# The SSD's decays between tokens: two float32r products over split log decays in place of one float32 product

## Chip, core and metric

The kernel runs on one core of a Trainium2 chip. The metric is the device time of one execution in microseconds (us), lower is better; the time before is the median of three runs. A profiled execution is taken beside these.

## The reference

A two-layer backbone over 1024 latent tokens and 256 context tokens, width 1024. Layer 0 has differential attention beside RWKV-7, layer 1 a bidirectional Mamba-2 SSD beside a bidirectional gated linear attention (GLA); each layer ends with a squared-ReLU MLP. What matters here is the SSD's chunk, of 128 tokens, for 8 heads and both directions:

```python
cum = jnp.cumsum(lac, axis=1)                       # log decays, summed along the tokens
lmat = jnp.exp(jnp.where(lower, cum[:, :, None] - cum[:, None, :], -jnp.inf))
cb = jnp.einsum('bign,bjgn->bijg', cc, bc)
xdt = xc * dtc[..., None]
y = jnp.einsum('bijgr,bjgrp->bigrp', cb[..., None] * lmat, xdt)
y = y + jnp.einsum('bign,bgrpn->bigrp', cc, h) * jnp.exp(cum)[..., None]
w_end = jnp.exp(cum[:, -1:] - cum)
h = h * jnp.exp(cum[:, -1])[..., None, None] + jnp.einsum('bjgn,bjgrp->bgrpn', bc, xdt * w_end[..., None])
```

`lmat` holds the decay between each two tokens: the exponential of the sum of the log decays that lie between them.

## The kernel before

Activations lie feature-major, 128 partitions wide. The large projections and the MLPs run as three float32r products of high and low parts (`mm3`, L87 to L89), with weights split on ACT (L95) and POOL (L99). Layer 1 goes in this order: projections with the SSD's convolution; the set-up of the SSD's log decays (`Ssd.dts`, about 2528 us), which fills `la`, one column per chunk, head and direction; the GLA's scores and its scan (`Gla.scan`, L1448 to L1497); the SSD's scan (`Ssd.scan`); the GLA's post-processing (`Gla.post`); the output projection `wout1`; the MLP. These stages overlap: the order of the instructions on each engine is planned when the kernel is built, by a list scheduler that uses its own cost model (`schedule_with_timeline_sim=True`), and then is fixed; each engine works through its own queue in order.

The SSD's scan takes nine or ten steps per direction over the chunks. A step updates the state (`xw` and the decayed state on POOL, L1176 and L1183; the product on PE, L1180; the sum on DVE, L1185), adds the part of the earlier chunks to the output (`inter`, L1244), and for each of the eight latent chunks calls `intra` (L1194) once. `intra` makes the decays between the tokens of the chunk in a PSUM tile `pd`, once for each group `g` of four heads, summed over both directions `d`. For a direction ACT writes `rl`, the mask `upto` or `from` scaled by the head's log decays (four instructions, L1221), and PE multiplies it by the mask `after` or `before` (L1222), a float32 product of 128x128 by 128x512. Then ACT takes the exponential (`G`, L1224), DVE multiplies by the masked scores (`us`, L1227) and PE multiplies by the values (L1232). That is 8 x 2 x 2 = 32 products at L1222 and 128 instructions at L1221. `rl` has two buffers.

`Gla.post` (L1499) runs through eight units. Each is a chain: squares on ACT (L1508), their sums on PE (L1511), an inverse square root by Newton steps on DVE (`rsqrt_newton`, L115 to L122), a broadcast on PE (L1515), two products on DVE (L1516, L1517) and a split on ACT and POOL. One PSUM buffer, `si`, carries both products of a unit.

`split` (L91) writes the high part by a copy that rounds to float32r and the low part as the difference.

## Time and profile before

| | |
|---|---|
| median of three runs | 3973.41 us (3969.83 to 3978.0) |
| the profiled execution | 3967.53 us |
| its span | 3965.7 us |
| PE busy | 3587.8 us, 90% of the span |
| DVE busy | 2048.2 us, 52% |
| POOL busy | 1305.6 us, 33% |
| ACT busy | 1138.8 us, 29% |
| mean granted TensorE clock | 0.935 of full speed |

The span runs from the first to the last instruction; the execution's time has 1.8 us more around it. Busy shares are means over stages with different limits, so the stage in which the changed lines run, about 2867 to 3056 us, is to be read by itself. A granted clock of 1.00 is 2.4 GHz, one of 0.50 is 1.2 GHz.

### The profile page before, as it was taken

The numbers are of one execution on the slowest core, as the hardware profiler recorded it, in microseconds if no ns is written. First come the engines' busy times: TensorE is split into PE (matmuls) and PEld (weight loads), VectorE is DVE, ScalarE is ACT, GpSimd is POOL, SyncE is SP. The second block draws the span as 40 slices with busy tenths as digits, with TensorE's granted clock in tenths as the row PEclk, the third lists the DMA queues.
The fourth block names the chain that finished last, engine by engine and source line by source line (L and its number), as shares of the span: only waits on it lengthen the run. The fifth ranks groups of instructions, "written<-read, shape, count | busy, mean of one in ns | idle before, by whom it ended". The sixth has DMA issues, their size and how long they took to land.

```text
span 3965.7 us, 68983 instructions
## 1 busy us (share of the span) xinstructions
PE 3587.8 (90%) x28912; PEld 2976.9 (75%) x28912; DVE 2048.2 (52%) x3741; ACT 1138.8 (29%) x1926; POOL 1305.6 (33%) x1121
## 2 busy tenths in 40 slices
PE   6999967766778879999999999999998889999998
PEld 4878846665667668888888888778776778888886
DVE  6344435766657647555444436357247663333335
ACT  3333321111255505111111113575543141111112
POOL 2455532322310015233222323217434352333223
PEclk8999977787788989999999999999999889999998
DMA  5244462333262142122222212232442311111111
GB/s 199 79 122 127 118 188 85 111 109 114 81 187 78 51 146 68 59 85 75 71 68 85 75 38 77 67 92 70 121 126 84 109 54 43 46 56 48 43 43 64
DMA packets 288999, 353.14 MB, mean 89 GB/s; under 512 B 91825, under 2 KB 217265, under 8 KB 288561
## 3 DMA queue, kind: packets, MB, share of 16 engines
q1 hardware_dynamic: 288688, 348.74, 28.3%
q8 instruction: 227, 3.72, 0.4%
q14 instruction: 84, 0.68, 0.1%
HBM read 265.03 MB, written 83.62 MB: 88 GB/s over the span
## 4 chain that ended last, share of the span: by engine, by line
PE 58%; DVE 3%; DMA 1%; ACT 1%; issue 1%; POOL 0%; SPq 0%; POOLq 0%; ACTq 0%; DVEq 0%
PE mm L87 10%; PE mm L88 10%; PE mm L89 10%; PE ss L87 4%; PE ss L88 4%; PE ss L89 4%; PE sp L88 4%; PE sp L87 4%; PE sp L89 4%; PE sp L1222 1%; PE ss L1475 1%; PE sp L1406 1%; PE si L1491 1%; PE mm L1232 1%; DMA wraw<-in_wout_dram 0%
## 5 line engine op out<-in xcount | busy, mean ns | idle before, releaser
L88 PE MATMUL mm<-actl,whi 128*128 128x512 f32 (+1 forms) x2432 | 903.3, 372 | 18.6 <-DVE actl L298 10.8
L87 PE MATMUL mm<-acth,whi 128*128 128x512 f32 (+1 forms) x2432 | 899.8, 372 | 19.2 <-ACT acth L95 6.9
L89 PE MATMUL mm<-acth,wlo 128*128 128x512 f32 (+1 forms) x2432 | 892.8, 370 | 0.0
L99 POOL TENSOR_TENSOR wlo<-wraw,whi 128x1024 fp32r<-128x1024 f32 (+2 forms) x243 | 495.7, 2047 | 1072.7 <-ACT whi L95 1065.4
L87 PEld LDWEIGHTS mm<-acth,whi 128*128 128x128 f32 x2432 | 465.1, 191 | 112.9 <-issue 8.1
L88 PEld LDWEIGHTS mm<-actl,whi 128*128 128x128 f32 x2432 | 465.3, 191 | 107.9 <-DVE actl L298 11.9
L89 PEld LDWEIGHTS mm<-acth,wlo 128*128 128x128 f32 x2432 | 465.0, 191 | 81.9 <-issue 4.4
L95 ACT CAST whi<-wraw 128x1024 fp32r<-128x1024 f32 (+2 forms) x243 | 217.1, 906 | 1049.5 <-PE mm L88 386.0
L345 POOL TENSOR_TENSOR relu<-relu 128x256 f32<-128x256 f32 (+1 forms) x163 | 162.2, 995 | 368.8 <-ACT relu L344 368.8
L97 DVE CAST hidh<-relu 128x256 fp32r<-128x256 f32 (+1 forms) x163 | 71.1, 436 | 354.8 <-POOL relu L345 353.6
L88 PE MATMUL sp<-hidl,whi 128*128 128x512 f32 (+1 forms) x648 | 238.5, 368 | 1.5 <-DVE hidl L99 1.5
L344 ACT ACTIVATE relu<-mm 128x256 f32<-128x256 f32 (+1 forms) x163 | 88.9, 545 | 520.8 <-PE mm L89 378.7
L87 PE MATMUL sp<-hidh,whi 128*128 128x512 f32 (+1 forms) x648 | 238.3, 368 | 0.0
L89 PE MATMUL sp<-hidh,wlo 128*128 128x512 f32 (+1 forms) x648 | 238.0, 368 | 0.0
L87 PE MATMUL ss<-hidh,whi 128*128 128x512 f32 (+1 forms) x600 | 222.8, 371 | 0.4 <-DVE hidh L97 0.4
L88 PE MATMUL ss<-hidl,whi 128*128 128x512 f32 (+1 forms) x600 | 222.5, 371 | 0.2 <-DVE hidl L99 0.2
L89 PE MATMUL ss<-hidh,wlo 128*128 128x512 f32 (+1 forms) x600 | 221.8, 370 | 0.0
L369 DVE SCALAR_TENSOR_TENSOR x<-ss,g,x 128x256 f32<-128x256 f32 x180 | 118.9, 661 | 145.2 <-PE ss L89 145.2
L369 DVE SCALAR_TENSOR_TENSOR x<-sp,g,x 128x512 f32<-128x512 f32 (+1 forms) x192 | 126.8, 661 | 105.5 <-PE sp L89 105.4
L220 DVE CUSTOM_DVE_ANT_0 mdj<-mdw,silu_r,t_cols 128x1024 f32<-128x1024 f32 x128 | 172.7, 1349 | 1.2
L369 DVE SCALAR_TENSOR_TENSOR x<-ss,g2b,x 128x512 f32<-128x512 f32 x120 | 90.0, 751 | 142.6 <-PE ss L89 142.6
L369 DVE SCALAR_TENSOR_TENSOR x<-sp,g2b,x 128x512 f32<-128x512 f32 (+1 forms) x132 | 96.7, 733 | 101.9 <-PE sp L89 101.9
(510 smaller groups left out, 6636.0 us busy)
## 6 DMA issues: line engine op xcount, KB each, us to landing
mdw<-in_modt_dram SPq DMA_DIRECT2D x80, 512.0 KB, 3.6
wraw<-in_wa_dram SPq DMA_DIRECT2D x64, 512.0 KB, 3.6
wraw<-in_wb_dram SPq DMA_DIRECT2D x64, 512.0 KB, 3.5
wraw<-in_win_dram SPq DMA_DIRECT2D x51, 512.0 KB, 3.8
x<-in_xT_dram SPq DMA_DIRECT2D x16, 640.0 KB, 10.7
rw_kr<-rw_t SPq DMA_DIRECT2D x16, 640.0 KB, 3.3
rw_bk<-rw_t SPq DMA_DIRECT2D x32, 320.0 KB, 3.9
rkr<-rw_kr SPq DMA_DIRECT2D x20, 512.0 KB, 5.1
```

Source lines behind the costliest of these rows:

```text
L87: self.nc.tensor.matmul(out, lh, rh, start=start and i == 0, stop=False)
L88: self.nc.tensor.matmul(out, lh, rl, start=False, stop=False)
L89: self.nc.tensor.matmul(out, ll, rh, start=False, stop=stop and i == n - 1)
L95: nc.scalar.copy(out=hi, in_=src)
L97: nc.vector.tensor_copy(out=hi, in_=src)
L99: e.tensor_tensor(out=lo, in0=src, in1=hi.bitcast(F32), op=ALU.subtract)
L220: nc.vector.tensor_tensor_reduce(out=junk, in0=raw, in1=rows[:, j], scale=1.0, scalar=modb[:, 8 * w + t : 8 * w + t + 1], op0=ALU.mult, op ...
L344: nc.scalar.activation(out=r, in_=ps, func=AF.Relu)
L345: nc.gpsimd.tensor_tensor(out=r, in0=r, in1=r, op=ALU.mult)
L369: nc.vector.scalar_tensor_tensor(out=xg, in0=ps, scalar=gate[:, m, j : j + 1], in1=xg, op0=ALU.mult, op1=ALU.add)
L1222: nc.tensor.matmul(pd, k["after" if d == 0 else "before"], rl.rearrange("p h t -> p (h t)"), start=d == 0, stop=d == 1)
L1232: nc.tensor.matmul(o, xd[d][:, hd * 64 : hd * 64 + 64], us[hd // 4, d][:, hd % 4], start=d == 0, stop=d == 1)
```

## The change

In the set-up `la` is split into a high part `lah`, rounded to float32r, and a low part `lal`, the rest, both as float32r tiles; the masks `after` and `before` are copied into float32r tiles `past[0]` and `past[1]`. In `intra` each `rl` becomes two tiles: the high one is written by ACT as before, with `lah` in place of `la`, and the low one by one GpSimd multiply of the mask with `lal`, over all four heads at once. Each float32 product then becomes two float32r products, of the high and of the low tile, added up in the same `pd`. Both new tiles have two buffers.

```diff
@@ Ssd.dts
+        self.lah, self.lal = (keep.tile([P, 10, 16], F32R, name=f"ss_la{x}") for x in "hl")
+        n.split(self.lah, self.lal, self.la)
+        self.past = [keep.tile([P, P], F32R, name=f"ss_past{d}") for d in range(2)]
+        for d in range(2):
+            nc.vector.tensor_copy(out=self.past[d], in_=k["after" if d == 0 else "before"])
+
@@ Ssd.intra
             for d in range(2):
-                rl = T([P, 4, P], "srl", 2)
+                rl = [self.pool.tile([P, 4, P], F32R, name=f"srl{x}", tag=f"srl{x}", bufs=2) for x in "hl"]
                 col = 8 * d + 4 * g
                 for r in range(4):
-                    nc.scalar.activation(out=rl[:, r], in_=tri[d], func=AF.Copy, scale=self.la[:, w + 2, col + r : col + r + 1])
-                nc.tensor.matmul(pd, k["after" if d == 0 else "before"], rl.rearrange("p h t -> p (h t)"), start=d == 0, stop=d == 1)
+                    nc.scalar.activation(out=rl[0][:, r], in_=tri[d], func=AF.Copy, scale=self.lah[:, w + 2, col + r : col + r + 1].bitcast(F32))
+                nc.gpsimd.tensor_tensor(out=rl[1], in0=tri[d].unsqueeze(1).to_broadcast([P, 4, P]),
+                                        in1=self.lal[:, w + 2, col : col + 4].bitcast(F32).unsqueeze(2).to_broadcast([P, 4, P]), op=ALU.mult)
+                for q, t in enumerate(rl):
+                    nc.tensor.matmul(pd, self.past[d], t.rearrange("p h t -> p (h t)"), start=d + q == 0, stop=d + q == 2)
```

## Rows read from the trace of the kernel before

**Rows 1.** The top of the page: the span and all instructions.

```profile
span 3965.7 us, 68983 instructions
```

**Rows 2.** Windows of the stage around the SSD's scan, every engine's busy time. Columns: stretch, its length, busy us of PE, PEld, DVE, ACT and POOL with the instructions in parentheses, granted TensorE clock, DMA share, GB/s.

```profile
2890.00:2940.00 50.00, 50.00 (x473) 36.14 (x473) 21.35 (x57) 22.54 (x87) 13.48 (x13) 1.00 0.37 109
2940.00:2991.00 51.00, 51.00 (x440) 36.52 (x441) 27.18 (x97) 17.95 (x47) 19.48 (x19) 1.00 0.40 116
2991.00:3042.00 51.00, 44.67 (x338) 32.95 (x337) 39.91 (x90) 23.66 (x61) 27.04 (x24) 1.00 0.30 89
```

**Rows 3.** The chain of work that ended last, in 2867 to 2991 us and in 2991 to 3042 us: shares of the stretch by engine, tile and line.

```profile
by line: PE ss L1475 20.5%; PE sp L1222 16.4%; PE si L1491 13.6%; PE mm L1232 12.3%; PE sp L1180 10.8%; PE mm L1257 7.9%; PE sp L1254 7.1%; PE ss L1477 7.0%; PE sp L1210 2.3%; ACT srl L1221 2.0%; DMA ss_z<-zg 1.8%; ACT gy L1483 0.2%; issue 
...
by line: PE sp L1222 16.1%; PE mm L1232 9.6%; PE mm L1257 8.9%; PE si L1511 8.5%; PE si L1515 8.4%; PE sp L1254 8.0%; DVE rsa_gl L120 5.8%; PE sp L1180 5.1%; DVE rsa_gl L121 4.7%; DVE rsy_gl L122 4.2%; DVE rsy_gl L116 3.2%; DVE rsyi_gl L115
```

**Rows 4.** The same kind of windows as rows 2, of L1222's instructions alone (PE, PEld, clock, DMA share, GB/s).

```profile
2867.00:2890.00 23.00, 4.50 (x8) 1.19 (x8) 0.78 0.67 197
2890.00:2940.00 50.00, 8.47 (x16) 2.54 (x16) 1.00 0.37 109
2940.00:2991.00 51.00, 8.47 (x16) 2.54 (x16) 1.00 0.40 116
2991.00:3042.00 51.00, 12.16 (x24) 3.86 (x24) 1.00 0.30 89
```

**Rows 5.** Pieces of the chain in one step of the SSD's scan: start, us on the chain, what, number of records.

```profile
2948.97 1.91 PE sp L1222 x4
...
2952.06 1.05 PE sp L1222 x2
```

**Rows 6.** First two pieces of the chain just ahead of the SSD's scan (columns as in rows 5), then the group of the same line in 2890 to 2991 us: line, engine, operation, tiles, shape, count | busy us, mean ns | idle before it.

```profile
2858.07 0.61 PE si L1491 x8
2859.41 0.67 PE si L1491 x8
...
L1491 PE MATMUL si<-gv,gkt 64*64 64x128 f32 x192 | 15.7, 282 | 0.0
```

**Rows 7.** A window of the second MLP, where PE does float32r products of 128x512 alone (columns as in rows 2), and the group of one of their weight loads in 3300 to 3360 us.

```profile
3300.00:3320.00 20.00, 20.00 (x88) 16.30 (x87) 9.33 (x14) 3.19 (x4) 6.92 (x5) 1.00 0.23 80
...
L87 PEld LDWEIGHTS mm<-acth,whi 128*128 128x128 f32 x44 | 8.3, 188 | 1.9
```

**Rows 8.** Groups of POOL in 2867 to 3060 us: count | busy us, mean ns | idle before them and what ended it.

```profile
L1183 POOL TENSOR_TENSOR sh<-sh,ss_dec 128x512 f32<-128x512 f32 x18 | 19.2, 1067 | 8.4 <-DMA gv<-gl_vt 8.2
...
L1242 POOL TENSOR_TENSOR sy<-sy,see 128x512 f32<-128x512 f32 x13 | 16.9, 1300 | 63.4 <-DVE see L1260 44.8 <-DMA gv<-gl_vt 12.4 <-DVE rsy_gl L116 3.4
```

**Rows 9.** POOL's instructions in order of time: start, busy us, line, operation, count, idle time ahead of it in brackets.

```profile
2940.09 1.27 POOL L1242 TENSOR_TENSOR sy<-sy,see 128x512 f32<-128x512 f32 x1 [13.16 <-DVE see L1260]
...
2943.34 2.04 POOL L1204 TENSOR_TENSOR sxd<-sxt,ss_dt 128x512 f32<-128x512 f32 x2
2947.48 1.04 POOL L1176 TENSOR_TENSOR sxw<-sxt,ss_wend 128x512 f32<-128x512 f32 x1 [2.10 <-PE sp L1180]
...
2961.94 1.27 POOL L1242 TENSOR_TENSOR sy<-sy,see 128x512 f32<-128x512 f32 x1 [12.43 <-DMA gv<-gl_vt]
...
3038.87 1.27 POOL L99 TENSOR_TENSOR ol<-gy,oh 128x512 fp32r<-128x512 f32 x1 [5.38 <-ACT oh L95]
```

**Rows 10.** L120 (a Newton step on DVE) in 2867 to 3082 us: shortest, median and longest in ns; then DVE and POOL in order of time.

```profile
L120 DVE TENSOR_TENSOR rsa_gl<-rsy_gl x24: 150/164/1266, 2995.4 to 3076.2; 128x4 f32<-128x4 f32 x24
...
3008.12 0.96 DVE L122 SCALAR_TENSOR_TENSOR rsy_gl<-rsa_gl,rsy_gl 128x4 f32<-128x4 f32 x1
...
3013.25 0.80 DVE L1517 TENSOR_TENSOR gy<-gy,gp_g 128x512 f32<-128x512 f32 x1
...
3007.02 2.04 POOL L1204 TENSOR_TENSOR sxd<-sxt,ss_dt 128x512 f32<-128x512 f32 x2
...
3013.45 1.50 POOL L1183 TENSOR_TENSOR sh<-sh,ss_dec 128x512 f32<-128x512 f32 x1
```

**Rows 11.** Pieces of the chain in 2991 to 3042 us around two of the GLA's norms, and the window of all of L1511's instructions there (eight to a unit).

```profile
3003.27 0.80 PE si L1511 x8
...
3011.28 1.16 PE si L1515 x8
...
3025.88 1.00 PE si L1511 x8
...
3034.54 1.16 PE si L1515 x8
...
2991.00:3042.00 51.00, 4.95 (x40) 5.01 (x40) 1.00 0.30 89
```

**Rows 12.** The group of L1221 in 2867 to 3060 us.

```profile
L1221 ACT ACTIVATE srl<-t_masks,ss_la 128x128 f32<-128x128 f32 x128 | 40.6, 390 | 24.0 <-PE sp L1222 19.8 <-DMA ss_z<-zg 4.0
```

**Rows 13.** The log decays' product in the set-up (shortest, median, longest in ns), and the window around the set-up's sums (columns as in rows 2).

```profile
L1134 DVE SCALAR_TENSOR_TENSOR ss_la<-ss_dt,ss_ea x1: 991/991/991, 2528.4 to 2528.4; 128x160 f32<-128x160 f32 x1
...
2530.00:2545.00 15.00, 15.00 (x75) 12.51 (x74) 0.71 (x3) 5.97 (x11) 2.34 (x1) 1.00 0.53 143
```

**Rows 14.** Windows of 4 us in the GLA's post-processing (columns as in rows 2).

```profile
3008.00:3012.00 4.00, 1.23 (x11) 1.04 (x10) 3.83 (x12) 0.00 (x0) 1.83 (x3) 1.00 0.57 166
...
3052.00:3056.00 4.00, 2.68 (x18) 2.69 (x18) 2.85 (x5) 1.23 (x2) 2.51 (x3) 0.81 0.47 129
3056.00:3060.00 4.00, 1.92 (x8) 1.54 (x8) 3.62 (x8) 1.14 (x2) 2.94 (x2) 0.50 0.22 66
```

## The prediction

> **What bounds the kernel now.** I read the page first, then the stage that the diff touches, in this order: the windows of the stage, the chain of work that ended last inside it, the instructions of the changed line, and then POOL, because the change gives POOL new work. The profiled span is 3965.7 us [rows 1]; its execution took 3967.53 us with what lies around it. The three timed runs lie higher, at a median of 3973.41 us. I make the sum against 3967.5 and carry the difference over to the median. A change below 0.2%, some 8 us, is about what this measurement cannot tell from none.
>
> The SSD's scan lies at about 2867 to 3056 us. It has two halves with different limits, which the reader is to see in the windows [rows 2]. From 2890 to 2991 PE is busy 101 of 101 us at a granted clock of 1.00 (2.4 GHz): the GLA's scan and the SSD's scan share TensorE there and nothing else is near full (DVE 48.5, POOL 33.0 us). From 2991 to 3042 PE is busy 44.7 of 51 us and DVE 39.9: the GLA's scan is over, and its post-processing, a serial chain of a sum of squares (L1511), a Newton square root on DVE (L115 to L122) and a broadcast (L1515), runs among the rest of the SSD. After 3042 no changed instruction is left, and what follows the chain (the last GLA units, then the SSD's own post) keeps its length wherever it starts.
>
> The changed line's product L1222 is on the chain. In 2867 to 2991 it is 16.4% of the chain, in 2991 to 3042 16.1% [rows 3]: of 124 us that is 20.3 us, of 51 us it is 8.2 us. The program makes 32 such products and the trace has 64 records of them, so two records are one product: 20 products before 2991 and 12 behind it [rows 4]. On the chain a product that stands alone takes 1.05 us, and two in a row take 1.91 us [rows 5]; so one costs 0.86 us, and the break behind a group 0.19 us.
>
> Is the dense half bound by PE, or by the serial GLA scan, in which a step waits for the state of the one before? In front of the SSD's start, with TensorE nearly to itself, two of its steps (L1491) follow each other in 1.34 us [rows 6], while in the dense half 192 records, eight to a step, that is 24 steps, share 101 us, 4.2 us each [rows 6]. It has slack of three to one, so PE time saved there is time saved.
>
> **The change part by part.**
>
> *Products.* For each of the 16 accumulations `pd`, two float32 products become four float32r products of the same 128x512 size. Such float32r products run at 88 in 20.0 us at full clock, 0.227 us each, with their weight loads (0.188 us) under them [rows 7]. Before 2991: 20.3 us for 10 accumulations, 2.03 us each. After: 4 x 0.227 = 0.91, and breaks. I take as many as now: 20.3 - 20 x 0.86 = 3.1 us, 0.31 per accumulation; so 1.22 us, and the gain is 10 x (2.03 - 1.22) = 8.1 us. If each low product is separated from its high one, two more breaks of 0.19 us for each accumulation take 3.8 us back: 4.3 to 8.1 us. I take 8.1, since a group is broken only where something is late and POOL has room in this half.
> Behind 2991: 8.2 us on the chain. At 0.91 us a product (8.2 us is nine) that is 4.5 accumulations, 5.5 us after, and the gain 2.7 us. Ends: 0, if the DVE part sets every step, and 6 x 0.81 = 4.9 us.
>
> *POOL's low parts.* Each of the 32 accumulation halves gets one GpSimd multiply of 128x512, both inputs repeated by a stride of zero. The nearest rows are multiplies with one repeated input, 1.04 us where nothing disturbs them (mean 1.07), and adds with two full ones, 1.27 us (mean 1.30) [rows 8, 9]; I take 1.04, as the operand shapes are those of the first kind, so 33 us over the stage. In the dense half 20 of them, 21 us, go on top of 33 of 101 us busy. In the order there, POOL finishes the `sxd` multiplies at 2945.4, has 2.1 us until the next state update, and after the two instructions of that update idles for 12.4 us, until 2961.9 [rows 9]; the first products of that step start at 2949.0, the next ones at 2952.1 [rows 5]. Two low parts, 2.1 us, fit ahead of the first pair and two behind: cost 0. If that cover is missed, PE stands before the low product for up to two POOL instructions, 2.1 us, in each of the eight calls.
> Behind 2991, 12 low parts, 12.5 us, go on top of 27.0 of 51 us. Here DVE pays: a Newton step of 128x4 has a minimum of 150 ns and a longest of 1266 ns [rows 10]. The reader is to see why in the rows from 3007 to 3009: beside POOL's instructions one such DVE step takes 0.96 us, about one POOL instruction; and at 3013 it goes the other way, a POOL multiply of 1.04 us takes 1.50 us beside a DVE product with two SBUF inputs [rows 10]. A POOL instruction inside a Newton chain therefore costs that chain about 0.96 - 0.16 = 0.8 us. The Newton steps of two of the units last 7.2 and 7.7 us, from the end of L1511 to the start of L1515 [rows 11], together 29% of the 51 us; if all five units that begin there (40 records of L1511, eight to a unit) were like them, 73%. I take half: 12 x 0.5 x 0.8 = 4.8 us, with ends 0 and 12 x 0.8 = 9.6 us. The Trainium skill, "SBUF — State Buffer", section "Who interferes with whom", says that a VectorE instruction with two SBUF inputs and a GpSimd instruction that reads SBUF exclude each other, the second waiting for the first to finish. By that rule alone the low parts cost what the rows at 3008 and 3013 show, and the trace agrees (0.96 in place of 0.16 us, 1.50 in place of 1.04 us); it is the ground of the second rival below.
>
> *ACT.* L1221 writes the high parts with the same shape, count and 390 ns [rows 12]; only its output type changes, and its longest waits are for the buffers that L1222 frees, which come free no later. 0, hidden by PE; ends 0 and 0.
>
> *Set-up.* The split of `la` and the two copies of the masks are three DVE instructions and one on POOL, none larger than the 0.99 us `la` product beside them, so at most 4 us. They fall where PE is busy 15.0 of 15 us with projections and POOL 2.3 [rows 13]: 0, hidden by these. Without that cover 4 us.
>
> *Order and memory.* The order of every engine is planned when the kernel is built, from the planner's own costs, and new tiles move the others in SBUF. No row prices a new order; the nearest is what one lone break costs, 0.19 us, so for each of the 32 new products between 0 and 6 us either way. I take 0.
>
> Sum: -8.1 - 2.7 + 4.8 = -6.0 us: 3961.5 us in the terms of the profiled execution, 3967 us in those of the median.
>
> **The rivals.**
> *The whole PE gain arrives.* The Newton chains miss the low parts, and the planner puts the shorter products where they close gaps: -8.1 - 2.7 to -8.1 - 4.9, so -11 to -13, and a few us of order: 3957 to 3963. For it: POOL has gaps of 5 us behind 2991 too [rows 9], and the GLA chain there is mostly PE. Against: DVE is busy 39.9 of 51 us.
> *POOL and DVE exclude each other.* All twelve late low parts fall into Newton chains: -8.1 - 2.7 + 9.6 = -1.2, with the breaks of the low products +2.6: 3972 to 3976. For it: the rows at 3008 [rows 10]. Against: low parts can run early, as they need only `la`, the masks and a free buffer.
> *POOL is late (slower).* POOL works in order, and its add into `y` (L1242) stood before a missing input for 12 to 13 us several times [rows 9]. A low part queued behind it, or behind two state updates, holds TensorE at the low product, and everything behind it. At 2.1 us in each of eight calls that is 16.6 us: -10.8 + 16.6 + 4.8 = +10.6, 3984. It decides from about 1.4 us per call on. For it: the first products come only 3.6 us behind the `sxd` multiplies. Against: the chains of [rows 3] list no wait for POOL, though TensorE has products that need POOL's state updates in every step.
> A fall of the clock belongs beside these: it stayed at 1.00 while PE was busy 1.23 of 4 us and went to 0.50 (1.2 GHz) behind a stretch of 2.68 of 4 us [rows 14]. Shorter products make PE idler, and if the fall came 10 us earlier PE's share of them, some 8 us, would take up to twice as long. It moves the forecast towards the second rival.
>
> **How the numbers follow.** Forecast (-3 to -10 us) 0.40; the whole gain 0.22; exclusion 0.21; POOL late 0.17. Over 0.2% faster are the whole gain and somewhat under half of the forecast's own range: 0.40. Within 0.2% the rest of it and the exclusion: 0.44. Slower by over 0.2%: most of the last rival, 0.16. The forecast's own range is 3963 to 3970. For 8 in 10 it reaches from the middle of the whole gain, 3958, to a POOL lateness of about half its price with the port's upper end, 3981.
>
> **What would show it.** Right: 64 records of L1222 at about 0.4 us, on the chain about 12 us before the end of the GLA's scan; that end at about 2983 in place of 2991; 32 POOL instructions of 1.04 us; L120 to L122 with a higher mean. Wrong: PE waiting for POOL at L1222's low product; PE idle in the dense half; a low-part multiply of 1.3 us or more; the clock at 0.50 before the last SSD step; or a different order of the GLA's post.

## The result, and the profile after

The changed kernel is slower. Its median is 4026.5 us (four runs, 4020.8 to 4028.0), that of the kernel before beside it 3971.6 us (four runs, 3966.8 to 3978.0). The ratio is 1.0136, with an interval of 1.0121 to 1.0151. Forecast were 3967 us and a range of 3958 to 3981.

The span of the profiled execution grew from 3965.7 us [rows 1] to 4026.2 us. Three stretches, read from the first and last starts of a tile's instructions, hold the difference. Ahead of the set-up, in code that is the same in both, 6.1 us had gone already, which lies within what two executions of one kernel differ by. The scan, from the first to the last product of the GLA that reads `gL` (L1475, now L1484), went from 129.8 to 166.3 us: +36.5. The post half, from the first sum of squares of the GLA (L1511, now L1520) to the last broadcast of the SSD's norms (L1280, now L1289), went from 185.2 to 203.3 us: +18.1. What follows is 788.1 us before and 787.8 after.

The windows of the changed kernel's scan, with the columns of [rows 2]:

```profile
2873.00:2896.00 23.00, 20.13 (x87) 16.05 (x87) 4.71 (x12) 7.72 (x33) 13.24 (x13) 0.50 0.63 185
2896.00:2946.00 50.00, 50.00 (x213) 38.75 (x212) 9.53 (x22) 12.08 (x47) 11.32 (x11) 0.50 0.19 55
2946.00:2997.00 51.00, 51.00 (x284) 40.32 (x285) 14.45 (x47) 9.96 (x37) 10.59 (x11) 0.61 0.22 62
2997.00:3035.00 38.00, 37.42 (x368) 28.09 (x364) 25.43 (x86) 16.32 (x44) 23.20 (x22) 1.00 0.46 130
```

PE is as busy as it was [rows 2]: 50 of 50 us. But the last number before the DMA share is the granted clock, 0.50 where it was 1.00, and in 50 us PE makes 213 products where it made 473. The busy column alone would call this stretch full; the clock and the count say that it ran at half speed. In windows of 4 us, first of the kernel before, then of the changed one, the reader sees where the clock falls and comes back:

```profile
2868.00:2872.00 4.00, 2.15 (x14) 2.15 (x15) 0.88 (x3) 2.16 (x12) 3.08 (x3) 0.50 0.84 243
2872.00:2876.00 4.00, 4.00 (x17) 2.72 (x17) 0.86 (x2) 0.51 (x4) 1.67 (x2) 0.50 0.75 218
2876.00:2880.00 4.00, 4.00 (x31) 2.78 (x31) 0.83 (x3) 0.65 (x4) 3.41 (x4) 0.87 0.79 226
```

```profile
2872.00:2876.00 4.00, 0.69 (x9) 0.44 (x9) 1.37 (x4) 2.83 (x12) 2.69 (x3) 0.64 0.75 238
2876.00:2880.00 4.00, 4.00 (x25) 3.55 (x26) 0.16 (x1) 0.68 (x5) 3.38 (x4) 0.50 0.87 252
...
2980.00:2984.00 4.00, 4.00 (x20) 3.37 (x20) 1.53 (x5) 0.00 (x0) 0.00 (x0) 0.50 0.15 45
2984.00:2988.00 4.00, 4.00 (x29) 2.54 (x27) 1.65 (x6) 0.00 (x0) 3.26 (x3) 0.78 0.34 85
```

In both, the first instructions of the SSD's scan wait for the last store of `z`, PE idles for a few microseconds and the clock falls to 0.50 (1.2 GHz) within them. Before, it is back after about 10 us. In the changed kernel PE is busy without a break from 2876 on and the clock stays at 0.50 to 2986, some 113 us. The groups of the changed lines in 2873 to 3125 us (columns as in [rows 8]):

```profile
L1484 PE MATMUL ss<-gL,gS 64*128 64x64 f32 x240 | 52.2, 360 | 3.3 <-ACT gy L1492 3.3
...
L1228 POOL TENSOR_TENSOR srll<-t_masks,ss_lal 128x512 fp32r<-128x512 f32 x32 | 34.7, 1094 | 37.4 <-PE sp L1231 30.1 <-DMA ss_z<-zg 7.3
...
L1231 PE MATMUL sp<-srlh,ss_past 128*128 128x512 f32 x32 | 17.7, 553 | 3.6 <-DVE sh L1191 2.6 <-DVE scm L1219 0.8
...
L1231 PE MATMUL sp<-srll,ss_past 128*128 128x512 f32 x32 | 15.9, 496 | 0.0
```

The 64 float32r products are busy for 33.6 us together, as long as the 32 old ones [rows 4], though many of them ran at half the clock. GpSimd's multiply takes 1.09 us, and it waits for PE (30.1 us), not PE for it. An unchanged product, L1484, shows where the loss is: 360 ns in place of 290 in the kernel before.

### The profile page after: what moved, and what is told of

Same layout as the page of the kernel before. It is cut to its first block, busy times and chain, and to the rows that moved or that the text cites. A ratio compares the mean times of both kernels' runs of the same rounds, so it can differ in the third digit from the quotient of the medians.

```text
span 4026.2 us, 69001 instructions
## 1 busy us (share of the span) xinstructions
PE 3643.4 (90%) x28912; PEld 3034.8 (75%) x28912; DVE 2058.5 (51%) x3744; ACT 1140.4 (28%) x1926; POOL 1340.4 (33%) x1154
## 4 chain that ended last, share of the span: by engine, by line
PE 58%; DVE 4%; DMA 1%; ACT 1%; issue 0%; POOL 0%; SPq 0%; POOLq 0%; ACTq 0%; DVEq 0%
PE mm L87 10%; PE mm L88 10%; PE mm L89 10%; PE ss L87 4%; PE ss L88 4%; PE ss L89 4%; PE sp L87 4%; PE sp L88 4%; PE sp L89 4%; PE ss L1484 1%; PE si L1500 1%; PE mm L1241 1%; PE sp L1415 1%; PE ss L1486 1%; PE sp L1231 0%
## 5 line engine op out<-in xcount | busy, mean ns | idle before, releaser
L97 DVE CAST hidh<-relu 128x256 fp32r<-128x256 f32 (+1 forms) x163 | 71.6, 439 | 356.7 <-POOL relu L345 355.5
```

Of the source, the lines that this page charges most:

```text
L97: nc.vector.tensor_copy(out=hi, in_=src)
```

## The experiments

The runs came in batches, each beside runs of the kernel before with medians of 3967 to 3973 us. "Clock back" is the time at which the granted clock leaves 0.50 after its fall at the start of the scan; where it falls once more inside the scan, that is said. "Scan" and "post half" are the stretches of the result section, from one profiled execution each. n/m is the number of `pd` accumulations ahead of and behind the end of the GLA's scan: 10/6 before, 8/8 in the changed kernel. Three theories stood at the start: the clock (it stays low because the start of the scan is different), the gap (the wait for `z` at the start makes it fall), and GpSimd's low parts (they hold up DVE or PE). The diffs are against the changed kernel unless they say otherwise.

### Two more products at the start

```diff
+            for _ in range(2 if w == 0 else 0):
+                nc.tensor.matmul(pd, k["after"], xt, start=True, stop=True)
             for d in range(2):
```

> The changed kernel with four extra float32 products of 128x512 in the first call of intra (two ahead of each pd, overwritten by the real ones): some 3.5 us more work for TensorE at full clock, the low parts still on POOL. Theory CLOCK (TensorE stays at 1.2 GHz from about 2874 to 2985 us of the changed kernel and this costs some 36 of its 55 us; one dense burst brings it to 2.4 GHz, where it stays): the granted clock is 1.00 within a few us behind the burst, the GLA's scan ends about 30 us earlier, 3985 to 3998 us in spite of the added work. Theory POOL (the low parts on POOL make TensorE wait, whatever the clock): nothing gained, 4028 to 4034 us.

Measured: 3990.7 us, ratio 1.0052 (1.0033 to 1.0071). Windows of 4 us:

```profile
2884.00:2888.00 4.00, 4.00 (x20) 3.33 (x18) 0.60 (x2) 0.33 (x2) 1.70 (x2) 0.50 0.39 115
2888.00:2892.00 4.00, 4.00 (x18) 2.04 (x18) 0.76 (x2) 0.17 (x2) 0.00 (x0) 0.75 0.23 66
2892.00:2896.00 4.00, 4.00 (x24) 2.52 (x20) 0.61 (x2) 2.55 (x12) 1.85 (x2) 1.00 0.18 49
```

Four idle float32 products of 512 columns, whose result is overwritten, take time and give 36 us back. The first of them starts at 2887.8; the clock is back at 2890, some 95 us earlier, but for a dip to 0.50 from 2917 to 2927, and the scan is 134.0 in place of 166.3 us. The post half keeps most of its loss (196.8 us, 10/6).

### The same, with the low parts on VectorE

Low parts on DVE for the first window of tokens only, then for all of them, then with the idle products of the run above for both head groups or for one, and with a third buffer for the high parts:

```diff
@@ low_dve_first
-                nc.gpsimd.tensor_tensor(out=rl[1], in0=tri[d].unsqueeze(1).to_broadcast([P, 4, P]),
+                (nc.vector if w == 0 else nc.gpsimd).tensor_tensor(out=rl[1], in0=tri[d].unsqueeze(1).to_broadcast([P, 4, P]),
@@ low_dve, low_dve_warm, low_dve_warm1, low_dve_bufs
-                nc.gpsimd.tensor_tensor(out=rl[1], in0=tri[d].unsqueeze(1).to_broadcast([P, 4, P]),
+                nc.vector.tensor_tensor(out=rl[1], in0=tri[d].unsqueeze(1).to_broadcast([P, 4, P]),
@@ low_dve_warm
+            for _ in range(2 if w == 0 else 0):
+                nc.tensor.matmul(pd, k["after"], xt, start=True, stop=True)
@@ low_dve_warm1
+            for _ in range(2 if w == 0 and g == 0 else 0):
+                nc.tensor.matmul(pd, k["after"], xt, start=True, stop=True)
@@ low_dve_bufs
-                rl = [self.pool.tile([P, 4, P], F32R, name=f"srl{x}", tag=f"srl{x}", bufs=2) for x in "hl"]
+                rl = [self.pool.tile([P, 4, P], F32R, name=f"srl{x}", tag=f"srl{x}", bufs=3 if x == "h" else 2) for x in "hl"]
```

> The changed kernel with the four low parts of the first call of intra made on DVE, the 28 others on POOL as before. On TensorE the planner then orders the SSD's first state products as in the kernel before. Theory CLOCK with the first order as its trigger: the clock rises at the start as in the kernel before, and about 36 us come back: 3980 to 3995 us. Theory POOL: seven eighths of the low parts remain, so 4018 to 4028 us. Theory CHEAP (the clock stays low because the float32r products themselves are too short, whatever the order): clock 0.50 for some 100 us again, 4020 to 4030 us.

> The changed kernel with all 32 low parts made on DVE, 0.69 us each if like the products of two SBUF inputs there (22 us over the stage), none on POOL. The planner's order of the first state products is that of the kernel before. Theory CLOCK: the clock rises in most runs as in the kernel before; DVE is the busier engine behind the GLA's scan and pays there 12 x 0.7 = 8 us at most: 3960 to 3975 us.

> The changed kernel with all low parts on DVE and the four extra float32 products in the first call of intra, overwritten by the real ones: the two remedies together. The planner leaves six accumulations behind the GLA's scan, as in the kernel before, in place of eight. If the 55 us are 36 of clock, 11 of order and 7 of POOL beside DVE, all three are gone but some 3.5 us of added work and a clock that rises a little later than before: 3950 to 3965 us, with little spread from run to run. If DVE's 22 us of low parts count behind the scan: 3965 to 3975 us.

> As low_dve_warm with two of the four extra products (those of the first pd alone). If two are enough to raise the clock: 2 us below low_dve_warm. If not: runs that lie 20 to 40 us apart, by when the clock comes back.

> The changed kernel with the low parts on DVE and three buffers for the high tile, no extra products: the planner leaves six accumulations behind the GLA's scan in place of the eight of low_dve, but splits the first state products by GLA products as in the changed kernel. Theory ORDER for the second half: the stretch from the GLA's first sum of squares to the SSD's last broadcast takes about 185 us in place of 197. Theory CLOCK for the first half: no burst, so the clock comes back late, and not in every run at the same time: 3955 to 4010 us.

| kernel | us | ratio | clock back | scan | post half | n/m |
|---|---|---|---|---|---|---|
| low_dve_first | 3975.7 | 1.0026 (0.9999 to 1.0053) | 2922 | 136.7 | 199.3 | 8/8 |
| low_dve | 3968.3 | 0.9998 (0.9982 to 1.0015) | 2922 | 135.9 | 196.7 | 8/8 |
| low_dve_warm | 3970.6 | 1.0007 (0.9998 to 1.0016) | 2877 | 116.1 | 193.7 | 10/6 |
| low_dve_warm1 | 3973.1 | 1.0006 (0.9990 to 1.0022) | 2887, a dip 2921 to 2931 | 131.8 | 192.1 | 10/6 |
| low_dve_bufs | 3989.3 | 1.0058 (1.0044 to 1.0071) | 2926 | 143.0 | 191.7 | 10/6 |

Where the clock is back after 10 us the scan is 116 us, 14 below the kernel before; where it is late by some 45 us, the scan is 136 to 143. The times of one program spread widely (low_dve 3961.9 to 3985.0 us, low_dve_first 3969.9 to 4024.1), so the profiled execution's clock need not be that of the median: low_dve's profiled execution is its slowest of ten. None of the five beats the kernel before. The expectation of low_dve_bufs on the post half, about 185 us at 10/6, failed: it is 191.7.

### Where the low parts are made, and where z is stored from

```diff
@@ low_act
-                nc.gpsimd.tensor_tensor(out=rl[1], in0=tri[d].unsqueeze(1).to_broadcast([P, 4, P]),
-                                        in1=self.lal[:, w + 2, col : col + 4].bitcast(F32).unsqueeze(2).to_broadcast([P, 4, P]), op=ALU.mult)
+                for r in range(4):
+                    nc.scalar.activation(out=rl[1][:, r], in_=tri[d], func=AF.Copy, scale=self.lal[:, w + 2, col + r : col + r + 1].bitcast(F32))
@@ z_act (and z_act_before, the same line in the kernel before)
-            nc.sync.dma_start(out=self.z[j][:, g0 - NCTX : g0 - NCTX + gn], in_=z)
+            nc.scalar.dma_start(out=self.z[j][:, g0 - NCTX : g0 - NCTX + gn], in_=z)
```

> The changed kernel with the low parts made on ACT, by 128 more instructions like those of the high parts (some 0.33 to 0.39 us each, 42 to 50 us over the stage); POOL and DVE get no new work. If what the low parts cost behind the GLA's scan is the exclusion of POOL and DVE, and the planner's order at the start is dense (two state products, one GLA product, two state products): clock back at 1.00 within some 10 us, 3955 to 3968 us. If ACT's order delays the exponentials and the GLA's copies: 3975 to 3995 us.

> The changed kernel with the store of the gate z issued from ACT's queue behind its own silu in place of SP's queue, where the last one stands 5.7 us behind loads of the GLA's scan; the first instructions of the SSD's scan wait for that store in every version. The low parts stay on POOL. Theory GAP (the clock falls because TensorE idles some 4 us at that wait, and then does not come back): the idle shrinks, the granted clock stays near 1.00 from 2870 us on, and the time falls to 3965 to 3985 us. Theory ORDER (the broken-up order of the small products cannot hold the clock, gap or none): 0.50 for tens of us all the same, 4000 to 4030 us.

> The kernel before, float32 products and all, with the store of z on ACT's queue as above. Theory GAP: the kernel before also loses some 8 us of full clock behind that wait (0.50 from 2868 to 2877 us) and idles 4 us; both shrink: 3962 to 3970 us. If the planner's new order costs as much: no change, 3970 to 3978 us.

low_act: 4004.3 us, ratio 1.0078 (1.0048 to 1.0108). That lies outside both expected ranges. The clock was back at 2879, fell again at 2886 with PE busy throughout, and stayed at 0.50 to about 2974; scan 158.9 us. No GpSimd low part exists here, so they are not needed for a long stay at 0.50.

z_act: 4014.9 us, ratio 1.0078 (1.0044 to 1.0111), but its ten executions fall into two groups, four of 3976 to 3980 us at a mean granted clock of 0.929 to 0.933, and six of 4014 to 4021 at 0.918 to 0.924. One program, with one order on every engine, is 38 us apart with the clock. That the clock's time is the loss, and not the order by itself, is shown most directly here. In the profiled execution, of the shorter group, the clock fell all the same though the store was issued early, and came back at 2899 (scan 127.4 us):

```profile
2864.00:2868.00 4.00, 3.42 (x18) 2.97 (x19) 1.43 (x5) 2.03 (x10) 3.30 (x4) 0.56 0.55 158
2868.00:2872.00 4.00, 4.00 (x26) 3.55 (x27) 0.60 (x2) 0.65 (x4) 1.05 (x2) 0.50 0.60 174
...
2896.00:2900.00 4.00, 4.00 (x23) 2.91 (x21) 1.29 (x2) 2.87 (x11) 3.36 (x4) 0.67 0.09 20
```

PE was busy 3.42 of 4 us in the window of the fall, and no pause in the ten microseconds ahead of it was longer than 0.9 us: the theory of the gap fails. z_act_before is the kernel before with nothing but that store moved: 3986.0 us, ratio 1.0042 (1.0029 to 1.0054). The planner gives it another order at the start, the clock is back at 2894 in place of 2877, and the scan takes 145.6 in place of 129.8 us. So a new order of the start costs time without a single float32r product: by half of the 17 us more at 0.50 some 9 of these 16 us are the clock, and the rest is not explained by it.

### One part of the change alone

```diff
@@ hi_only
-                nc.gpsimd.tensor_tensor(out=rl[1], in0=tri[d].unsqueeze(1).to_broadcast([P, 4, P]),
-                                        in1=self.lal[:, w + 2, col : col + 4].bitcast(F32).unsqueeze(2).to_broadcast([P, 4, P]), op=ALU.mult)
-                for q, t in enumerate(rl):
-                    nc.tensor.matmul(pd, self.past[d], t.rearrange("p h t -> p (h t)"), start=d + q == 0, stop=d + q == 2)
+                nc.tensor.matmul(pd, self.past[d], rl[0].rearrange("p h t -> p (h t)"), start=d == 0, stop=d == 1)
@@ split_f32
-                rl = [self.pool.tile([P, 4, P], F32R, name=f"srl{x}", tag=f"srl{x}", bufs=2) for x in "hl"]
+                rl = [self.pool.tile([P, 4, P], F32, name=f"srl{x}", tag=f"srl{x}", bufs=2) for x in "hl"]
...
-                    nc.tensor.matmul(pd, self.past[d], t.rearrange("p h t -> p (h t)"), start=d + q == 0, stop=d + q == 2)
+                    nc.tensor.matmul(pd, k["after" if d == 0 else "before"], t.rearrange("p h t -> p (h t)"), start=d + q == 0, stop=d + q == 2)
@@ pool_only (against the kernel before, whose float32 products stay; lal is made in the set-up)
+                low = self.pool.tile([P, 4, P], F32R, name="srll", tag="srll", bufs=2)
+                nc.gpsimd.tensor_tensor(out=low, in0=tri[d].unsqueeze(1).to_broadcast([P, 4, P]),
+                                        in1=self.lal[:, w + 2, col : col + 4].bitcast(F32).unsqueeze(2).to_broadcast([P, 4, P]), op=ALU.mult)
```

> The changed kernel without the low parts: one float32r product of the high part per direction, no GpSimd multiply (the low part of each log decay is left out of the sums between tokens). Theory CLOCK with order as trigger: the clock rises as in the kernel before, TensorE has 32 x (0.86 - 0.23) = 20 us less to do, of which 13 before the GLA's end: 3955 to 3965 us. Theory POOL: the same time, 3955 to 3965, but the clock says nothing. Theory CHEAP: the clock stays at 0.50 for some 100 us, 4000 us or more.

> The kernel before with the split of the log decays and the 32 low parts on POOL added, written into a tile that nobody reads; the float32 products are as in the kernel before. Theory POOL: most of the 55 us, 4010 to 4030 us, with the clock at 1.00 through the scan. Theory CLOCK with order as trigger: the planner's order at the start is broken up as in the changed kernel, but the float32 products of 0.86 us come a few us later and raise the clock there: low for 10 to 30 us, 3980 to 4000 us. Theory CHEAP: the clock rises as in the kernel before, and only POOL's share of DVE costs: 3975 to 3985 us.

> The changed kernel, POOL's low parts and all, with the high and low parts as float32 tiles and float32 products: 64 products of 0.86 us in place of 64 of 0.23, some 40 us more for TensorE at full clock than the changed kernel. Theory CHEAP (the short float32r products are part of why the clock does not come back): the clock is at 1.00 within some 20 us as in pool_only, and the time falls all the same or stays: 3995 to 4015 us. Without that (the order alone): the clock stays low for about 100 us again, 4050 us or more.

hi_only, which leaves the low parts out of the sum: 3952.1 us, ratio 0.9950 (0.9932 to 0.9968), clock back at 2880, scan 112.2, post half 185.4 us. split_f32: 4004.5 us, 1.0095 (1.0079 to 1.0110), 9/7, clock back at 2894, scan 148.1, post half 195.8. pool_only: 3981.0 us, 1.0026 (1.0014 to 1.0038), clock back at 2894, scan 147.0, post half 187.0. In the two with float32 products, as in z_act_before, the clock came back after 20 to 27 us, although the order at the start is a new one. The stays of 55 to 113 us (the changed kernel, low_act, low_dve, low_dve_first, low_dve_bufs, and hi_pool below) all belong to kernels whose decays are float32r products with no idle float32 products ahead of them. That alone does not make a long stay, as hi_only shows.

### Zeros in place of the low parts, and low parts that nobody reads

Both leave the low parts out of the sum.

```diff
@@ hi_zero (hi_zero_warm: with the idle products of warm_first too)
+        self.zlow = pool.tile([P, 4, P], F32R, name="szl", tag="szl", bufs=1)
+        nc.vector.tensor_scalar(out=self.zlow, in0=self.k["upto"].unsqueeze(1).to_broadcast([P, 4, P]), scalar1=0.0, scalar2=None, op0=ALU.mult)
...
-                rl = [self.pool.tile([P, 4, P], F32R, name=f"srl{x}", tag=f"srl{x}", bufs=2) for x in "hl"]
+                rl = [self.pool.tile([P, 4, P], F32R, name="srlh", tag="srlh", bufs=2), self.zlow]
...
-                nc.gpsimd.tensor_tensor(out=rl[1], in0=tri[d].unsqueeze(1).to_broadcast([P, 4, P]),
-                                        in1=self.lal[:, w + 2, col : col + 4].bitcast(F32).unsqueeze(2).to_broadcast([P, 4, P]), op=ALU.mult)
@@ hi_pool
-                for q, t in enumerate(rl):
-                    nc.tensor.matmul(pd, self.past[d], t.rearrange("p h t -> p (h t)"), start=d + q == 0, stop=d + q == 2)
+                nc.tensor.matmul(pd, self.past[d], rl[0].rearrange("p h t -> p (h t)"), start=d == 0, stop=d == 1)
```

> The second product reads one constant tile of zeros: the low parts of the log decays are left out, all 64 float32r products stay, GpSimd makes nothing of them. If the post half's +18 us comes from the low parts' making (GpSimd beside VectorE, or the wait for it), the post half is 185 to 188 us. If it comes from the number of products and their order (8 accumulations before and 8 behind the end of the scan, as in the changed kernel), it is 193 us or more. The scan depends on the clock: about 112 us if the clock is back within 15 us, 135 or more if not; the whole is 3950 to 3990.

> The low parts are made on GpSimd and no product reads them: they are left out of the sum, which has the high product alone, as hi_only. If GpSimd beside VectorE costs the post half what was lost, it is 193 us or more against hi_only's 185.4; if it costs what the float32 kernel with unread low parts showed (187.0 against 185.2), it is 185 to 188. The scan is 112 us if the clock comes back as early as in hi_only, 130 or more if not.

> As hi_zero (the low parts are left out, their products read zeros), with the SSD's state and decay products put ahead of the GLA's small ones at the start, as in the kernel before. If the clock's late return is the small products' place at the start, it is back by about 2890, the scan is 112 to 120 us and the whole is under hi_zero's by what hi_zero's clock came later. If the post half follows the number of accumulations behind the scan, it lies within 3 us of hi_zero's.

hi_zero: 3957.5 us, ratio 0.9988 (0.9962 to 1.0015); scan 115.7, post half 186.1 us, 8/8; its ten executions go from 3949.0 to 4000.9 us, and the profiled one is the fastest. hi_zero_warm: 3958.2 us, 0.9972 (0.9958 to 0.9987); 115.4 and 187.6 us. hi_pool: 3988.8 us, 1.0064 (1.0047 to 1.0080); 149.7 and 185.9 us. Two windows of hi_zero:

```profile
2880.00:2970.00 90.00, 90.00 (x814) 69.26 (x812) 43.45 (x144) 36.39 (x126) 22.90 (x22) 1.00 0.40 117
...
2974.80:3055.80 81.00, 71.60 (x584) 56.88 (x583) 71.31 (x152) 36.10 (x91) 43.72 (x38) 0.98 0.34 103
```

and of the changed kernel, the same two stages:

```profile
2880.00:2980.00 100.00, 100.00 (x444) 78.44 (x444) 19.04 (x48) 23.69 (x92) 22.64 (x22) 0.50 0.23 66
...
3035.10:3134.40 99.30, 80.11 (x577) 66.28 (x578) 74.58 (x149) 36.13 (x89) 56.36 (x51) 0.82 0.25 76
```

In the scan PE makes 9.04 products a microsecond at 1.00 and 4.44 at 0.50, from the same lines, and both kernels are 8/8. At 0.50 for some 110 us in place of hi_zero's 10, the changed kernel loses about half of 100, and its scan is 50.6 us longer. With all 64 float32r products and eight accumulations behind the scan its post half is 186.1 us, as before; the clock there, 0.98, was higher than in the kernel before, as the windows further down show. hi_pool ran at 0.50 from 2866 to 2940 without a single low product:

```profile
2876.00:2936.00 60.00, 59.28 (x265) 47.72 (x261) 18.75 (x32) 15.85 (x61) 43.64 (x42) 0.50 0.30 87
...
2940.00:2944.00 4.00, 4.00 (x38) 3.20 (x37) 1.90 (x4) 2.20 (x9) 0.00 (x0) 0.93 0.06 18
```

The whole scans, from the first to the last product that reads `gL`, of the kernel before, the changed one, low_dve and hi_zero:

```profile
2860.50:2990.30 129.80, 125.75 (x1084) 89.83 (x1084) 56.58 (x173) 51.84 (x179) 42.47 (x41) 0.96 0.44 129
...
2866.70:3033.00 166.30, 162.49 (x994) 126.71 (x996) 54.32 (x166) 45.52 (x158) 56.35 (x54) 0.66 0.32 94
...
2860.60:2996.50 135.90, 134.62 (x994) 105.10 (x996) 63.00 (x184) 44.84 (x158) 38.20 (x36) 0.79 0.39 115
...
2857.20:2973.00 115.80, 111.39 (x985) 85.78 (x986) 50.74 (x164) 43.65 (x157) 35.95 (x34) 0.96 0.44 129
```

The length of a scan times its mean granted clock estimates what it would take at full clock: 125 us in the kernel before, 110, 107 and 111 in the three others. In all fifteen kernels whose decays are float32r products (those of the next experiment too) it is 107 to 119 us, while the scans themselves take 112 to 166; in the four with float32 products it is 125 to 138. So at full clock the changed kernel's scan would be some 15 us shorter than the one before, and the some 102 us more at 0.50 (113 against 10) cost half of that, 51 us: together about the +36.5.

hi_pool's expectation on the post half told nothing apart, as it turned out. Nobody reads its low parts, so GpSimd started the last of them at 2928, ahead of the post half (in pool_only at 2918).

So the second pair of windows, the GLA's norms from the first to the last sum of squares, is where the low parts have to be compared. The whole +18.1 us lies in it (81.2 us before, 99.3 after; the rest of the post half is 104.0 in both). The groups of the Newton steps on DVE there, in the changed kernel and in hi_zero:

```profile
L121 DVE SCALAR_TENSOR_TENSOR rsa_gl<-rsa_gl,rsm_gl 128x4 f32<-128x4 f32 x21 | 10.7, 509 | 0.6
L120 DVE TENSOR_TENSOR rsa_gl<-rsy_gl 128x4 f32<-128x4 f32 x21 | 9.2, 437 | 0.6
...
L122 DVE SCALAR_TENSOR_TENSOR rsy_gl<-rsa_gl,rsy_gl 128x4 f32<-128x4 f32 x21 | 6.4, 305 | 0.6
...
L116 DVE TENSOR_SCALAR rsy_gl<-rsyi_gl 128x4 int32<-128x4 int32 x7 | 5.3, 761 | 0.2
```

```profile
L120 DVE TENSOR_TENSOR rsa_gl<-rsy_gl 128x4 f32<-128x4 f32 x21 | 8.3, 397 | 0.7
L122 DVE SCALAR_TENSOR_TENSOR rsy_gl<-rsa_gl,rsy_gl 128x4 f32<-128x4 f32 x21 | 8.2, 391 | 0.6
L121 DVE SCALAR_TENSOR_TENSOR rsa_gl<-rsa_gl,rsm_gl 128x4 f32<-128x4 f32 x21 | 7.5, 356 | 0.6
...
L116 DVE TENSOR_SCALAR rsy_gl<-rsyi_gl 128x4 int32<-128x4 int32 x7 | 2.4, 339 | 0.2
```

With L115 (2.8 and 2.5 us) the Newton steps take 34.4 us in the changed kernel, 28.9 in hi_zero, 28.2 before. In the five kernels whose GpSimd makes low parts there (after, warm_first, low_dve_first, z_act, split_f32) they take 32.9 to 36.4 us; in the fourteen others, 22.0 to 31.9 (77 instructions in each). Instruction by instruction the changed kernel's trace shows why: two GpSimd instructions that make low parts (in one line), and three Newton steps, of which the first two lie beside them:

```profile
3054.48 2.04 POOL L1228 TENSOR_TENSOR srll<-t_masks,ss_lal 128x512 fp32r<-128x512 f32 x2
...
3054.58 0.96 DVE L120 TENSOR_TENSOR rsa_gl<-rsy_gl 128x4 f32<-128x4 f32 x1
3055.58 0.96 DVE L121 SCALAR_TENSOR_TENSOR rsa_gl<-rsa_gl,rsm_gl 128x4 f32<-128x4 f32 x1
3056.57 0.16 DVE L122 SCALAR_TENSOR_TENSOR rsy_gl<-rsa_gl,rsy_gl 128x4 f32<-128x4 f32 x1
```

Of the 77, the 44 that lie beside no GpSimd instruction take 0.16 us in the mean, the 14 beside a low part 0.83, the 19 beside another GpSimd instruction 0.82; before, 54 lie beside none and 23 beside one. That is the exclusion of GpSimd and VectorE, at about 6 us. PE waits 12.0 us for the end of a Newton chain there (L122), 8.1 us before and 4.7 us in hi_zero.

The other 12 us are not settled. Against hi_zero, PE is busy 80.1 us at 0.82 for 577 products where hi_zero's 584 take 71.6 us at 0.98: 8.5 of the +18.3 us are a slower PE, and 9.8 an idler one. But a low clock alone does not lengthen this stretch. The same windows of the kernel before, of hi_only, and of hi_zero_warm and warm_first, which both have the idle products:

```profile
2992.40:3073.60 81.20, 67.49 (x484) 51.77 (x482) 60.70 (x142) 29.13 (x70) 36.92 (x32) 0.88 0.28 83
...
2978.40:3060.40 82.00, 66.33 (x474) 54.09 (x474) 61.51 (x143) 29.44 (x70) 36.74 (x33) 0.81 0.28 83
...
2971.10:3054.60 83.50, 70.83 (x541) 57.16 (x540) 69.82 (x146) 30.04 (x72) 43.05 (x37) 0.88 0.30 88
...
3000.60:3093.20 92.60, 71.73 (x505) 56.88 (x504) 70.39 (x143) 30.53 (x72) 50.66 (x45) 0.86 0.27 77
```

hi_only took 82.0 us at 0.81, with fewer products. So hi_zero, at 0.98, does not show that two more accumulations behind the scan are free; its clock may have hidden their price. With the clock nearly equal and no more products, warm_first, whose low parts are made, is 9.1 us longer than hi_zero_warm, which has none. And the low parts cost without GpSimd as well: low_dve and low_bf16_nw (below) make them on DVE, and their stretches are 93.4 and 95.3 us. What the waits for low parts, the two accumulations and the clock each cost in the changed kernel, and whether the lower clock made the chain longer or the waits made the clock fall, these runs do not tell.

### Cheaper low parts

```diff
@@ low_bf16 (new lines only, against low_dve_warm; low_bf16_nw is the same against low_dve)
+        self.past16, self.tri16 = ([keep.tile([P, P], mybir.dt.bfloat16, name=f"ss_{x}{d}") for d in range(2)] for x in ("p16", "t16"))
+        for d in range(2):
+            nc.vector.tensor_copy(out=self.past16[d], in_=k["after" if d == 0 else "before"])
+            nc.vector.tensor_copy(out=self.tri16[d], in_=k["upto" if d == 0 else "from"])
...
+                rl = [self.pool.tile([P, 4, P], t, name=f"srl{x}", tag=f"srl{x}", bufs=2) for x, t in (("h", F32R), ("l", mybir.dt.bfloat16))]
...
+                for r in range(4):
+                    nc.vector.tensor_scalar(out=rl[1][:, r], in0=self.tri16[d], scalar1=self.lal[:, w + 2, col + r : col + r + 1].bitcast(F32),
+                                            scalar2=None, op0=ALU.mult)
...
+                    nc.tensor.matmul(pd, (self.past, self.past16)[q][d], t.rearrange("p h t -> p (h t)"), start=d + q == 0, stop=d + q == 2)
```

> All of the sum is kept; the low parts, the second matrix of zeros and ones and the second mask are bfloat16, each low part is four VectorE operations of 128 columns, and two idle products stand in front of the first decays, as in low_dve_warm. If the post half's loss is the product's wait for its low part, and the four short operations together take less than the 0.68 us of the one float32r operation, the post half is 187 to 192 us against 193.7; if they take as long or longer, 193 or more. With the clock back by about 2880 the scan is near 116 us and the whole 3958 to 3968, against 3967 to 3973 of the kernel before; with a late clock 3975 or more.

> As low_bf16 without the two idle products at the start. The post half is low_bf16's within 3 us. If the idle products are what brings the clock back early, the scan is 130 us or more and the whole 3965 to 3990; if float32r products alone are no hindrance when their low parts come early, it is 116 us, and the whole is low_bf16's.

Measured: 3972.4 us, ratio 1.0000 (0.9985 to 1.0016), scan 125.8, post half 191.4 us; and 3971.6 us, 1.0015 (0.9998 to 1.0032), 116.6 and 198.7 us. The low part's group in low_bf16:

```profile
L1235 DVE TENSOR_SCALAR srll<-ss_t,ss_lal x128: 242/251/1320, 2876.7 to 3047.2; 128x128 bf16<-128x128 bf16 x128
```

The four short operations are not cheaper: 0.251 us each, 1.0 us together, against 0.68 us for the one of 512 columns in float32r; the 191.4 us lie in the range that was expected of cheaper ones, without its ground. The expectation that the idle products set the clock fails here: without them the clock was back at 2884, some 10 us after its fall, with them at 2900, some 24 us after it. What the second expected of the post half fails as well: 7.3 us apart, at 8/8 against 10/6, so an accumulation behind the scan may cost something once its low part has to be made there; the clock differs too, by a little (0.82 against 0.84 in the norms). No kernel that keeps the whole sum beat the one before. The two that point that way, hi_only and hi_zero_warm, leave the low parts out.

## Why the prediction was wrong, point by point

**Products: right in direction, and larger.** Where the clock came back as early as before, the scan is 116.1 us (low_dve_warm, with the ten accumulations ahead of its end that the step counted) against 129.8, a gain of 13.7 us where the step "Before 2991" said 8.1: 1.4 us for each, not 0.81, and low_dve_warm's four idle products lie in its scan besides. The mechanism is right and its term is too small. hi_only has one float32r product in place of one float32 product, and its scan times its clock is 107 us against 125: an estimate of 0.9 us for each of the 20, where [rows 5] and [rows 7] give 0.86 - 0.23 = 0.63. So the pieces of [rows 5] seem to undercount what a float32 product costs PE; the orders differ too, and no run measures it alone.

**Order and memory: the step that failed.** It said "between 0 and 6 us either way. I take 0", priced from a lone break of 0.19 us. It looked at gaps on PE, and there are none: PE is busy 100 of 100 us. What the term left out is that the clock's return after its fall at the start can move: from 10 us to 113, and the scan came out 36.5 us longer where the sum had it 8.1 shorter. The sum also took 10/6 as given; the planner made it 8/8, two more accumulations for the post half. What makes the clock's return late stays open. The planned order of the start was, before, two and two state products (L1180) around one group of L1491 and four pairs of the GLA's small products, then the products of L1210. In the changed kernel the state products come in pairs between small ones, and the L1210 products singly. Of the kernels with the first order, five were back after 10 to 14 us (hi_only, hi_zero, hi_zero_warm, low_dve_warm, low_bf16_nw), two after 24 (low_dve_warm1, low_bf16), and two after 55 to 58 (low_dve, low_dve_first). None of those with small products in between was back in under 20 us, and three of them took 58 to 113 (low_dve_bufs, hi_pool, the changed kernel). So the order may be one part, and it is not all of it: in the profiled executions of low_dve and hi_zero PE's instructions come in the same order at the start, with a product of zeros for the low one, and the clock was back after 58 us in one and 10 in the other.

**The clock: seen, and mispriced.** The prediction set a fall beside the rivals, in the late stage, at "some 8 us". [rows 14] were read for what idleness does; the windows of 4 us at the start of the scan, in the same trace, show 0.50 for 10 us, in the later ones with PE at 4.00 of 4, and were not read. The changed kernel shows that PE being busy was not enough to bring the clock back. A stay in the scan, where PE is the limit, costs half its length, and this one was 113 us. Of the +36.5 us it is all and more: hi_zero's scan stands 14.1 us under that of the kernel before, the changed kernel's 50.6 us above hi_zero's.

**POOL and DVE: right, in mechanism and in size.** 4.8 us were summed for the Newton steps; they grew by 6.2 against before. The Trainium skill, "SBUF — State Buffer", section "Who interferes with whom", on whose rule that rival stood, is borne out here by which engine makes the low parts: 33 to 36 us of Newton steps with GpSimd, 22 to 32 without. But the stage, forecast at -2.7 + 4.8 = +2.1 us, lost 18.1. The sum had no term for the other 12: it had six accumulations there in place of eight, and no wait for a low part. Which of these and of the clock (0.82 against 0.88 before) they are stays open.

**POOL late: did not come.** In the changed kernel PE's waits for GpSimd at L1231 come to 0.2 us, none of it for a low part, and GpSimd waits 30.1 us for PE. L1228 took 1.09 us for the forecast 1.04. The rival's side, slower, was right and its mechanism was not.

**What was named as the sign of an error** held: the clock at 0.50 before the last SSD step. The product's share of the chain in the scan did fall, from 16.4% [rows 3] to 9.1% of 2873 to 3035 us, while the end came at 3033 in place of the forecast 2983.

## What to carry to other kernels

Making PE's work shorter or putting it in another order can cost more through the granted clock than it saves. Ahead of such a change read the clock and the count of products in windows of a few microseconds wherever it falls, not only the busy column, and where TensorE is the limit price a late return at half its length. A planner's new order is a part of every change, and a kernel with only a moved store can show its price. If a part is to be made on another engine, look for the serial chain it will lie beside.

## What the hardware showed

A busy TensorE stayed at 0.50 (1.2 GHz) for some 113 us, with 100 of 100 us busy and 444 products where 904 fit at full clock; before, it left 0.50 after 10 us. The Trainium skill, "TensorE: Matmul & The Clock Gate", section "What's actually happening", lets the clock follow how busy the engine has lately been. By that rule PE would have been back at full clock soon after 2876, and the scan would have been some 116 us. Here the trace does not agree as far as the profile's busy column goes, which counts modelled time: PE was at 4.00 of 4 us in every window from 2876 to 2984, at 0.50. The same page, section "Seeing it yourself", warns that records of the clock can be wrong; here the count of products halves with them.

One program had two times 38 us apart (z_act), with the granted clock of 0.93 and 0.92 in the mean. Four idle products of 512 columns ahead of the first decays took 36 us off the changed kernel, and in the low_bf16 pair they took nothing off: the effect depends on what else is in the queue, and no rule for it was found here.
